# First MoE: token rows fetched from DRAM by index, and output rows carried to the tokens through DRAM

## The chip, the cores and the metric

One Trainium2 chip, one NeuronCore. The metric is the device time of one execution in microseconds (us), the median of three runs. Engines are called as in the profile: PE (TensorE), DVE (VectorE), ACT (ScalarE), POOL (GpSimd), SP (the engine that issues the weight loads).

## What is computed

A two-block network on 256 tokens of width 1024; the second block also carries 256 context tokens. Each layer of the second block ends in a mixture of experts (MoE). The change is in the first of the two, which works on all 512 tokens:

```python
def moe(h, router_w, router_b, w_gate, w_up, w_down):   # 16 experts, hidden width 512, 2 experts per token
    scores = jax.nn.sigmoid(t @ router_w)
    ...                                                 # best group of 4 experts, the best 2 in it
    wts = wts / jnp.sum(wts, axis=-1, keepdims=True)
    def expert(acc, p):
        wg, wu, wd, gate_col = p
        y = (jax.nn.silu(t @ wg) * (t @ wu)) @ wd
        return acc + gate_col[:, None] * y, None
```

The gate and up weights of one expert are 1024x512 f32 each (2 MB), its down weights 512x1024 (2 MB): 96 MB for the 16 experts, all read from DRAM once.

## The kernel before

Only the tokens that chose an expert are sent through it. `route` and `plan` score the tokens, order the experts by their load and give each token a slot number in each expert that it chose. The work is cut into tiles of 128 slots. A tile "B" is one expert with 128 slots; a tile "P" is a pair of experts with 64 slots each. `ORDER` lists the 12 tiles of this MoE (`BBBPBPBPBPBB`), and two neighbours make a unit: B B, four times B P, B B. An expert with more tokens than slots gets further rounds in a branch (`overflow`), which all engines pass between `plan` and the first unit.

For each unit:
- `gather`: DVE writes one-hot matrices `m_oh` (token by slot). For each of 8 chunks of 128 features, PE multiplies them with the normalised tokens, which are kept as a rounded part `m_xh` and a rest `m_xl`: 8 x 4 x 2 = 64 matmuls of 256 columns. ACT and DVE bring the result to `m_u0` and `m_u1`. Eight small matmuls with `m_w2` give the weight of each slot (`m_wsl`).
- `hidden`: gate and up products (PSUM `up`). A B tile splits its weights into a rounded part and a rest on ACT (L249, `phi`) and DVE (L250, `plo`) and takes three products (`acc3`); a P tile multiplies in full f32 straight from the loaded weights `wraw`. Four transposes turn the result.
- `down`, `down2`: the down product (PSUM `pd`) and `outputs`, which scales it into `m_y`, again as a rounded part and a rest.
- `combine`: two matmuls with `m_sP` and two DVE compares make the transposed one-hot `m_ot`; `scatter` multiplies it with `m_y` (32 matmuls of 512 columns), and 16 DVE operations add the result to the tokens `xl` and `xc` (L2067).

Weights come in 1 MB loads on SP's queue (`wraw`) into a ring of six buffers; a buffer is free again when it has been split (B) or multiplied (P). The loop over the jobs (one for each tile) runs `hidden` of job n, `combine` of the unit that is done, `gather` of the next unit, then `down` of job n-1. A scheduler puts the instructions of each engine in a fixed order when the program is built; it interleaves these groups on PE, but each engine then runs in that order.

Of the kernel before, what the change touches and what calls it, by code (L numbers as in the profile page):

```python
# [6 lines left out]
F32 = mybir.dt.float32  # L7
F32R = mybir.dt.float32r
I32 = mybir.dt.int32
AF = mybir.ActivationFunctionType  # L10
OP = mybir.AluOpType
AX = mybir.AxisListType
# [3 lines left out]
NCH = 8  # L16
# [136 lines left out]
class Kern:  # L153
# [1547 lines left out]
    def plan(self, asg, sc, nt, mp):  # L1701
# [3 lines left out]
        N = 128 * nt  # L1705
# [54 lines left out]
        for j in range(nt):  # L1760
            self.mm(pv[:, 16 * j:16 * j + 16], wT[:, 128 * j:128 * j + 128], pm.bitcast(F32), True, True)
        w2 = mp.tile([128, nt, 16, 2], F32R, name="m_w2")
        pv = pv[:, :16 * nt].rearrange("p (a b) -> p a b", b=16)
# [37 lines left out]
    def moe(self, l, seqs):  # L1801
# [30 lines left out]

        y = self.big0.tile([128, 2, 2, 1024], F32R, name="m_y")
        xh = self.big0.tile([128, nt, 1024], F32R, name="m_xh")
        xl = self.big0.tile([128, nt, 1024], F32R, name="m_xl")
# [36 lines left out]

        st = {"n": 0}
        for j in range(nt):
            s, ts = j // 2, slice(128 * (j % 2), 128 * (j % 2) + 128)
            for q in range(2):
                n = 2 * j + q
                tp = self.pp.tile([128, 512], F32, name="aux" if n in (4, 5) else "mm", bufs=3 if n in (4, 5) else 4)
                sl = slice(512 * q, 512 * q + 512)
                for i in range(4):  # L1880
                    self.mm(tp[:, 128 * i:128 * i + 128], seqs[s][0][:, 4 * q + i, ts], gain[:, s, 4 * q + i], i == 0, False)
                self.mm(tp, ri[:, j % 2, s], shift[:, s, sl], False, True)
                st["xh"] = nc.scalar.activation(xh[:, j, sl], tp, AF.Copy, scale=rk[:, s, j % 2:j % 2 + 1])
                if l == 0 and n < 6:
                    v = mp.tile([128, 512], F32, name="m_xv", bufs=2)
                    nc.scalar.activation(v, tp, AF.Copy, scale=rk[:, s, j % 2:j % 2 + 1])
                    nc.gpsimd.tensor_tensor(xl[:, j, sl], v, xh[:, j, sl].bitcast(F32), OP.subtract)
                else:
                    nc.vector.scalar_tensor_tensor(xl[:, j, sl], tp, rk[:, s, j % 2:j % 2 + 1], xh[:, j, sl].bitcast(F32), op0=OP.mult, op1=OP.subtract)
        idr = mp.tile([16, 16], F32R, name="m_idr")  # L1890
        nc.vector.tensor_copy(idr, C["ident"][:16, :16])
# [46 lines left out]
        def gather_(oh, u):  # L1938
# [7 lines left out]
            for c in range(NCH):  # L1946
# [9 lines left out]
                for t in range(n):  # L1956
# [4 lines left out]
                    if not all(plain):  # L1961
                        nc.vector.tensor_tensor(xs[t][:, c], xs[t][:, c], xp[:, 1, t], OP.add)
            wps = aux()[:, :8 * n].rearrange("p (t w) -> p t w", t=n)
            wsl = mp.tile([128, 2], F32, name="m_wsl", bufs=2)
            for t, es in enumerate(u):
                for j in range(nt):
                    self.mm(wps[:, t, :2 * len(es)], oh[:, j, t], w2[:, j, es[0]:es[0] + len(es)].rearrange("p a b -> p (a b)"), j == 0, j == nt - 1)
                k = 128 // len(es)
                for e in range(len(es)):
                    nc.vector.tensor_reduce(wsl[k * e:k * e + k, t:t + 1], wps[k * e:k * e + k, t, 2 * e:2 * e + 2], AX.X, OP.add)  # L1970
            return wsl

        def gather(u):
            oh = mp.tile([128, nt, 2, 128], F32R, name="m_oh")
            for t, es in enumerate(u):
                n, k = len(es), 128 // len(es)
                if n > 1:
# [4 lines left out]
            return gather_(oh, u)  # L1982

# [37 lines left out]
        def outputs(pds, t, wsl):  # L2021

            yo, ws = y[:, t], wsl[:, t:t + 1]
            for z in range(2):
                cs = slice(512 * z, 512 * z + 512)
                nc.scalar.activation(yo[:, 0, cs], pds[z], AF.Copy, scale=ws)  # L2026
                nc.vector.scalar_tensor_tensor(yo[:, 1, cs], pds[z], ws, yo[:, 0, cs].bitcast(F32), op0=OP.mult, op1=OP.subtract)  # L2027

        up_ps()
# [27 lines left out]
        def scatter(ot):  # L2057

            for c in range(NCH):
                op = aux()  # L2060
                n = 0
                for i, o in enumerate(ot):
                    for v in range(2):
                        self.mm(op[:, :N], y[:, i, v, 128 * c:128 * c + 128], o, n == 0, n == 2 * len(ot) - 1)
# [56 lines left out]
        ws = gather(units[0])  # L2121
        st["late"], st["n"] = (st["xh"], st["oh"]), 0
        pend = done = None
# [28 lines left out]

    def run_all(self):
        with self.wpool(3) as self.wp, self.tc.tile_pool(name="xp", bufs=1, reuse_waits="tile") as self.xp:
            with self.tc.tile_pool(name="mwp", bufs=1, reuse_waits="tile") as self.mwp:
# [4 lines left out]
        with self.wpool(3) as self.wp:  # L2160
            self.layer2()
        self.moe_consts()
        with self.wpool(6) as self.wp, self.phase() as self.big0, self.phase() as self.big:
            self.moe(0, [(self.xl, 0), (self.xc, 1)])
# [36 lines left out]
```

## Time and profile before

| | |
|---|---|
| time, median of 3 runs | 2230.29 us (2228.47 to 2234.14) |
| profiled execution | 2234.03 us, span 2232.3 us |
| PE busy in the span | 2122.1 us (95%) |
| DVE busy | 1429.5 us (64%) |
| ACT busy | 1007.4 us (45%) |
| POOL busy | 72.7 us (3%) |
| DMA | 425.12 MB moved, mean 190 GB/s |

The span runs from the first to the last instruction of the profiled execution; what lies around it makes 1.7 us more. Busy shares are means over stages with different limits: the first MoE is one such stage, and the rows below are read from it.

### The profile page before, as it was taken

Reading aid. Unit: us, or ns where it says so; the run is one execution under the profiler, and the core shown is the slowest. Engines: PE = TensorE matmul, PEld = TensorE weight load, DVE = VectorE, ACT = ScalarE, POOL = GpSimd, SP = SyncE. Lnnn points to the kernel's source line nnn. Section 1 sums busy time; section 2 is a strip of 40 time slices with the busy share of each in tenths; the row PEclk is TensorE's granted clock in tenths of the full one; section 3 lists DMA queues with packets and bytes.
Section 4 is the critical chain, followed back from the end, with each engine's and each line's share of the span. In section 5 each row is a group of like instructions: output and inputs, shape, how many; then the busy total and the mean of one; then the engine's idle time right before and its main releaser. Section 6 shows DMA issues by size and latency. Waiting matters only on the chain. (4 is left out here: it accounts for less than half of the span.)

```text
span 2232.3 us, 34618 instructions
## 1 busy us (share of the span) xinstructions
PE 2122.1 (95%) x13602; PEld 1648.4 (74%) x13602; DVE 1429.5 (64%) x2749; ACT 1007.4 (45%) x1769; POOL 72.7 (3%) x131
## 2 busy tenths in 40 slices
PE   7999999999999999999799899999989999989997
PEld 6999788678998778778567587655678899754442
DVE  5886566657876789999774476543767678631222
ACT  5564534445555454555433474332546465221111
POOL 0100100110100000000000100000000000000000
PEclk9999989999999999999899999999999999989999
DMA  7765753546645222211012368888634343469996
GB/s 276 268 256 191 257 188 119 210 166 232 241 158 187 81 67 76 67 57 48 21 38 76 124 234 310 321 320 299 235 122 141 97 151 106 152 265 394 425 395 246
DMA packets 78166, 425.12 MB, mean 190 GB/s; under 512 B 12256, under 2 KB 14048, under 8 KB 38048
## 3 DMA queue, kind: packets, MB, share of 16 engines
q1 hardware_dynamic: 74912, 422.32, 51.6%
q8 instruction: 110, 1.80, 0.3%
q0 software_dynamic: 3072, 0.40, 0.1%
q14 instruction: 72, 0.59, 0.1%
HBM read 421.24 MB, written 1.05 MB: 189 GB/s over the span
## 5 line engine op out<-in xcount | busy, mean ns | idle before, releaser
L197 PE MATMUL mm<-act_x,whi 128*128 128x256 f32 x2048 | 383.5, 287 | 0.9 <-DVE act_x L352 0.4
L197 PEld LDWEIGHTS mm<-act_x,whi 128*128 128x128 f32 x2048 | 323.4, 193 | 22.9 <-issue 18.6
L197 PE MATMUL mm<-act_x,wlo 128*128 128x256 f32 x1024 | 292.1, 286 | 0.8 <-DVE wlo L228 0.8
L197 PE MATMUL mm<-act,phi 128*128 128x512 f32 (+2 forms) x816 | 264.4, 399 | 6.3 <-ACT phi L249 3.5
L228 DVE TENSOR_TENSOR wlo<-wraw,whi 128x2048 fp32r<-128x2048 f32 (+1 forms) x101 | 208.3, 2063 | 88.8 <-ACT whi L227 88.4
L227 ACT CAST whi<-wraw 128x2048 fp32r<-128x2048 f32 (+1 forms) x101 | 173.7, 1720 | 178.8 <-PE mm L197 133.8
L250 DVE TENSOR_TENSOR plo<-wr,phi 128x1024 fp32r<-128x1024 f32 (+2 forms) x146 | 159.2, 1095 | 103.7 <-ACT phi L249 102.1
L249 ACT CAST phi<-wr 128x1024 fp32r<-128x1024 f32 (+2 forms) x146 | 137.4, 943 | 194.3 <-PE mm L197 165.0
L197 PEld LDWEIGHTS mm<-act_x,wlo 128*128 128x128 f32 x1024 | 197.7, 193 | 4.3 <-issue 2.7
L197 PEld LDWEIGHTS mm<-act,phi 128*128 128x128 f32 (+1 forms) x816 | 150.6, 189 | 46.5 <-issue 8.6
L197 PE MATMUL up<-wraw,m_u 128*64 128x512 f32 (+2 forms) x744 | 184.3, 596 | 0.0
L1038 DVE SCALAR_TENSOR_TENSOR uc<-up,fvt,uc 128x512 f32<-128x512 f32 x217 | 158.9, 746 | 7.5 <-ACT uc L1033 6.2
L197 PE MATMUL mm<-act,plo 128*128 128x512 f32 (+2 forms) x408 | 161.8, 398 | 0.0
L197 PE MATMUL mm<-act_x,phi 128*128 128x256 f32 x768 | 147.7, 292 | 3.5 <-ACT qs L1528 3.0
L197 PEld LDWEIGHTS up<-wraw,m_u 128*64 128x64 f32 (+2 forms) x744 | 58.9, 137 | 100.8 <-issue 100.0
L197 PEld LDWEIGHTS mm<-act_x,phi 128*128 128x128 f32 x768 | 124.1, 198 | 7.8 <-ACT qs L1528 3.2
L250 DVE TENSOR_TENSOR plo<-wraw,phi 128x1024 fp32r<-128x1024 f32 x96 | 114.3, 1221 | 11.6 <-ACT phi L249 10.4
L249 ACT CAST phi<-wraw 128x1024 fp32r<-128x1024 f32 x96 | 99.2, 1055 | 43.6 <-DMA wraw<-in_moe_d_dram 14.9
L197 PE MATMUL mm<-act_x,plo 128*128 128x256 f32 x384 | 111.9, 292 | 2.1 <-DVE plo L250 2.0
L2008 DVE TENSOR_TENSOR m_g<-m_g,up 128x512 f32<-128x512 f32 x20 | 13.7, 687 | 135.5 <-PE up L197 135.5
L197 PE MATMUL mm<-hhi,whi 128*128 128x256 f32 x352 | 99.7, 284 | 0.0
L197 PE MATMUL mm<-hlo,whi 128*128 128x256 f32 x352 | 99.7, 284 | 0.0
(609 smaller groups left out, 4276.4 us busy)
## 6 DMA issues: line engine op xcount, KB each, us to landing
wraw<-in_moe_g_dram SPq DMA_DIRECT2D x64, 1024.0 KB, 6.8
wraw<-in_moe_u_dram SPq DMA_DIRECT2D x61, 1024.0 KB, 8.8
wraw<-in_moe_d_dram SPq DMA_DIRECT2D x61, 1024.0 KB, 9.1
wmod<-in_mod_w_dram SPq DMA_DIRECT2D x48, 1024.0 KB, 6.1
wraw<-in_ffn_up_dram SPq DMA_DIRECT2D x44, 1024.0 KB, 4.9
wr<-in_hg_in_dram SPq DMA_DIRECT2D x64, 512.0 KB, 3.9
wraw<-in_ffn_down_dram SPq DMA_DIRECT2D x32, 704.0 KB, 4.0
wraw<-in_ple_gate_dram SPq DMA_DIRECT2D x8, 1024.0 KB, 4.9
```

What stands on the lines that cost most here:

```text
L197: self.nc.tensor.matmul(out, lhsT, rhs, start=first, stop=last)
L227: nc.scalar.copy(hi, raw)
L228: nc.vector.tensor_tensor(lo, raw, hi.bitcast(F32), OP.subtract)
L249: self.nc.scalar.copy(hi, src)
L250: self.nc.vector.tensor_tensor(lo, src, hi.bitcast(F32), OP.subtract)
L1038: nc.vector.scalar_tensor_tensor(o, up[:, :, k:k + 64], self.fv("cf_w", 8 * k + b), o, op0=OP.mult, op1=OP.add)
L2008: nc.vector.tensor_tensor(sg, sg, u, OP.mult)
```

## The change

Only the first MoE changes (`rowed`). Two DRAM tensors are new: `xd` holds the 512 normalised tokens as rows of 4 KB, `yd` the output rows of the first ten tiles and one row of zeros.
- Ahead of the units, ACT writes each of the eight token pieces a second time in f32 (`m_xv`, two buffers; six pieces did so before) and POOL stores it to `xd`. DVE works out for each token the two rows of `yd` that will hold its outputs (`r_rowi`).
- `m_w2` has two more columns, a token number and zero, so that the eight small matmuls also give the token number of each slot.
- The first unit is gathered as before. For each later unit, `ask` makes the one-hot and the small matmuls one tile ahead and lets POOL fetch 128 token rows for each of its two tiles by an indirect transfer (`xg`, two buffers). `fetch` turns them with 16 PE transposes and splits (B) or copies (P) them to `m_u0` and `m_u1`.
- `outputs` of the first ten tiles writes f32 rows (`y0`, four buffers), and POOL stores them to `yd`. Their `combine` is gone. In the last job `collect` fetches for each block of 128 tokens the two rows of each token (eight indirect transfers), adds them on DVE, turns them with 32 transposes and adds them to `xl` and `xc`.
- The last unit keeps its `combine`.

The new tiles `xg`, `yg` and `y0` take the places of `m_xh`, `m_xl` and `m_y`. The diff, cut to its core:

```diff
-        w2 = mp.tile([128, nt, 16, 2], F32R, name="m_w2")
+        w2 = mp.tile([128, nt, 16, nt], F32R, name="m_w2")
+        if nt == 4:
+            tn = mp.tile([128, nt, 2], F32, name="r_tn")
+            nc.vector.memset(tn[:, :, 1], 0.0)
+            for j in range(nt):
+                nc.vector.tensor_scalar(tn[:, j, 0:1], self.pidx[:, 0:1], float(128 * j - self.SLOT), None, op0=OP.add)
+            nc.vector.tensor_copy(w2[:, :, :, 2:], tn[:, :, None].to_broadcast([128, nt, 16, 2]))
...
+        rowed = l == 0
+        if rowed:
+            xd = self.dram.tile([128 * nt, 1024], F32, name="xd")
+            yd = self.dram.tile([128 * (len(order) - 2) + 1, 1024], F32, name="yd")
+            none = 128 * (len(order) - 2)
...
-                if l == 0 and n < 6:
+                if rowed:
                     v = mp.tile([128, 512], F32, name="m_xv", bufs=2)
                     nc.scalar.activation(v, tp, AF.Copy, scale=rk[:, s, j % 2:j % 2 + 1])
-                    nc.gpsimd.tensor_tensor(xl[:, j, sl], v, xh[:, j, sl].bitcast(F32), OP.subtract)
+                    nc.gpsimd.dma_start(xd[128 * j:128 * j + 128, sl], v)
+                    (nc.gpsimd if n < 6 else nc.vector).tensor_tensor(xl[:, j, sl], v, xh[:, j, sl].bitcast(F32), OP.subtract)
...
+            nc.vector.tensor_tensor(e, slot, bc(1), OP.is_lt)
+            nc.vector.scalar_tensor_tensor(e, slot, float(self.SLOT), e, op0=OP.is_ge, op1=OP.mult)
+            nc.vector.tensor_tensor(v, slot, bc(0), OP.add)
+            nc.vector.tensor_tensor(v, v, e, OP.mult)
+            rows = mp.tile([128, 2, nt], F32, name="r_rows")
+            nc.vector.tensor_reduce(rows[:, 0], v, AX.X, OP.min)
+            nc.vector.tensor_tensor(e, v, rows[:, 0][:, :, None].to_broadcast([128, nt, 16]), OP.is_equal)
+            nc.vector.scalar_tensor_tensor(v, e, 1e5, v, op0=OP.mult, op1=OP.add)
+            nc.vector.tensor_reduce(rows[:, 1], v, AX.X, OP.min)
+            nc.vector.tensor_scalar(rows, rows, 0.0, float(none), op0=OP.min, op1=OP.add)
+            rowi = mp.tile([128, 2, nt], U32, name="r_rowi")
+            nc.vector.tensor_copy(rowi, rows)
...
+        def slots_(oh, u, idx=None):
+            n = len(u)
+            wps = aux()[:, :4 * nt * n].rearrange("p (t w) -> p t w", t=n)
...
                 for j in range(nt):
-                    self.mm(wps[:, t, :2 * len(es)], oh[:, j, t], w2[:, j, es[0]:es[0] + len(es)].rearrange("p a b -> p (a b)"), j == 0, j == nt - 1)
+                    self.mm(wps[:, t, :nt * len(es)], oh[:, j, t], w2[:, j, es[0]:es[0] + len(es)].rearrange("p a b -> p (a b)"), j == 0, j == nt - 1)
...
+            if idx is not None:
+                nc.vector.tensor_copy(idx, wps[:, :n, 2])
...
+        def ask(u):
+            ti = mp.tile([128, 2], U32, name="m_ti", bufs=2)
+            wsl = slots_(onehot(u), u, ti)
+            k = st["asked"] = st.get("asked", 1) ^ 1
+            for t in range(2):
+                nc.gpsimd.indirect_dma_start(xg[:, k, t], None, xd[:, :], bass.IndirectOffsetOnAxis(ap=ti[:, t:t + 1], axis=0))
+            return u, k, wsl
+        def fetch(asked):
+            u, k, wsl = asked
+            xs = []
+            for t, es in enumerate(u):
+                p = whole(es)
+                v = mp.tile([128, 1024 if l == 1 else 2048], F32 if p else F32R, name="m_u%d" % t)
+                v = v[:, :1024].rearrange("p (c n) -> p c n", c=NCH) if p else v.rearrange("p (c v n) -> p c v n", c=NCH, v=2)
+                xs.append(v)
+                for q in range(2):
+                    tp = aux()
+                    for i in range(4):
+                        c = 4 * q + i
+                        nc.tensor.transpose(tp[:, 128 * i:128 * i + 128], xg[:, k, t, 128 * c:128 * c + 128], C["ident"])
+                    tp = tp.rearrange("p (c n) -> p c n", c=4)
+                    o = v[:, 4 * q:4 * q + 4]
+                    if p:
+                        nc.scalar.copy(o, tp)
+                    else:
+                        self.split(o[:, :, 0], o[:, :, 1], tp)
+            st["x"] = xs
+            return wsl
...
-            yo, ws = y[:, t], wsl[:, t:t + 1]
+            ws = wsl[:, t:t + 1]
+            i = st["tile"]
+            st["tile"] += 1
+            if 0 <= i < len(order) - 2 and rowed:
+                yo = y0[:, i % 4]
+                nc.scalar.activation(yo[:, :512], pds[0], AF.Copy, scale=ws)
+                nc.vector.tensor_scalar(yo[:, 512:], pds[1], ws, None, op0=OP.mult)
+                nc.gpsimd.dma_start(yd[128 * i:128 * i + 128], yo)
+                return
+            yo = st["y"][:, t]
...
+        def collect():
+            for s_, (x, r) in enumerate(seqs):
+                for j in range(2):
+                    J = 2 * s_ + j
+                    for k in range(2):
+                        nc.gpsimd.indirect_dma_start(yg[:, j, k], None, yd[:, :], bass.IndirectOffsetOnAxis(ap=rowi[:, k, J:J + 1], axis=0))
+                    nc.vector.tensor_tensor(yg[:, j, 0], yg[:, j, 0], yg[:, j, 1], OP.add)
+                for q in range(4):
+                    tp = aux().rearrange("p (c j t) -> p c j t", c=2, j=2)
+                    for i in range(2):
+                        c = 2 * q + i
+                        for j in range(2):
+                            nc.tensor.transpose(tp[:, i, j], yg[:, j, 0, 128 * c:128 * c + 128], C["ident"])
+                        nc.vector.scalar_tensor_tensor(x[:, c], tp[:, i].rearrange("p j t -> p (j t)"), self.mvec(l, 5, c, r), x[:, c], op0=OP.mult, op1=OP.add)
...
+        if rowed:
+            xg, yg = (self.big0.tile([128, 2, 2, 1024], F32, name=v) for v in ("m_xh", "m_xl"))
+            y0 = self.big0.tile([128, 4, 1024], F32, name="m_y")
+            nc.gpsimd.memset(y0[0:1, 3], 0.0)
+            nc.gpsimd.dma_start(yd[none:none + 1], y0[0:1, 3])
+        pend = done = asked = None
         for n in range(len(jobs) + 1):
             if n < len(jobs):
                 u, t = jobs[n]
                 hd = hidden(u[t], t)
                 next(hd)
                 now, last = (u, t, ws), t + 1 == len(u)
+                if rowed and t == 0 and n + 2 < len(jobs):
+                    asked = ask(jobs[n + 2][0])
             if done:
                 combine(done)
                 done = None
+            if rowed and n == len(jobs) - 1:
+                collect()
             if n + 1 < len(jobs) and last:
-                ws = gather(jobs[n + 1][0])
+                ws = fetch(asked) if rowed else gather(jobs[n + 1][0])
             if pend:
                 (u_, t_, w_), hT, l_ = pend
+                if rowed and st["tile"] == len(order) - 2:
+                    st["y"] = self.big0.tile([128, 2, 2, 1024], F32R, name="m_y")
                 if whole(u_[t_]):
                     down2(u_[t_], hT, t_, w_)
                 else:
                     down(u_[t_][0], hT, t_, w_)
-                if l_:
+                if l_ and not (rowed and u_ is not units[-1]):
                     done = u_
```

## Rows read from the trace of the kernel before

**Rows 1.** Busy time of each engine in three stretches (the columns stand in its first line):

```profile
core 0: us, PE busy (x) PEld busy (x) DVE busy (x) ACT busy (x) POOL busy (x), PEclk, DMA share, GB/s
2040.00:2130.00 90.00, 89.84 (x392) 39.13 (x389) 14.64 (x32) 11.46 (x29) 0.00 (x0) 1.00 1.01 425
1436.80:1496.70 59.90, 59.90 (x286) 35.91 (x284) 29.82 (x50) 19.87 (x36) 0.00 (x0) 1.00 0.82 306
1592.00:1627.00 35.00, 33.58 (x146) 26.50 (x145) 32.37 (x49) 20.60 (x26) 0.00 (x0) 1.00 0.37 136
```

**Rows 2.** Timeline of PE: start, duration, instruction, count, idle time before and its releaser:

```profile
1282.37 1.01 PE L197 MATMUL aux<-m_oh,m_xh 128*128 128x256 f32 x3 [2.87 <-ACTq L2106]
...
1429.16 0.64 PE L197 MATMUL aux<-m_oh,m_xh 128*128 128x256 f32 x4
...
1436.83 0.50 PE L197 MATMUL aux<-m_w,m_oh 128*128 128x2 f32 x4
...
1443.22 0.60 PE L2012 MATMUL aux<-c_ident,m_g 128*128 128x128 f32 x4
1443.58 0.47 PE L197 MATMUL up<-phi,m_u 128*128 128x512 f32 x1
...
1454.93 7.09 PE L197 MATMUL pd<-wraw,m_hT 128*64 128x512 f32 x32
...
1466.12 0.49 PE L197 MATMUL aux<-m_sP,m_idr 16*128 16x512 f32 x1
...
1466.77 1.07 PE L197 MATMUL up<-wraw,m_u 128*64 128x512 f32 x2
...
1496.62 0.50 PE L197 MATMUL aux<-m_w,m_oh 128*128 128x2 f32 x4
...
1620.64 7.46 PE L197 MATMUL aux<-m_ot,m_y 128*128 128x512 f32 x32
1628.04 0.64 PE L197 MATMUL aux<-sq,c_ones 128*32 128x256 f32 x8
```

**Rows 3.** DMA issues from 1282 to 1640: count, KB of each, median us to landing:

```profile
wraw<-in_moe_g_dram SPq DMA_DIRECT2D x30, 1024.0 KB, 6.5
wraw<-in_moe_u_dram SPq DMA_DIRECT2D x30, 1024.0 KB, 6.7
wraw<-in_moe_d_dram SPq DMA_DIRECT2D x30, 1024.0 KB, 5.4
```

**Rows 4.** Timeline of SP's queue, first and last loads of one B P unit:

```profile
1432.82 14.54 SPq L214 DMA_DIRECT2D wraw<-in_moe_d_dram  x4
...
1488.82 1.17 SPq L214 DMA_DIRECT2D wraw<-in_moe_u_dram  x2
```

**Rows 5.** Two stretches of 5 us of the first MoE, columns as in the first group:

```profile
1282.00:1287.00 5.00, 4.63 (x22) 4.63 (x23) 3.32 (x3) 4.39 (x7) 0.14 (x1) 0.52 0.01 5
...
1307.00:1312.00 5.00, 5.00 (x23) 4.04 (x22) 4.65 (x6) 4.00 (x6) 0.00 (x0) 1.00 1.00 357
```

**Rows 6.** Groups of instructions from 1436.8 to 1496.7 (one B tile's splits):

```profile
L250 DVE TENSOR_TENSOR plo<-wraw,phi 128x1024 fp32r<-128x1024 f32 x12 | 14.4, 1224 | 2.0 <-ACT phi L249 1.7
```

**Rows 7.** Timelines of ACT, DVE and POOL ahead of the first unit:

```profile
1263.17 0.68 ACT L1886 ACTIVATE m_xv<-mm,r_rk 128x512 f32<-128x512 f32 x1
...
1270.99 0.57 ACT L1717 CAST m_g<-aux 16x512 fp32r<-16x512 f32 x1 [3.67 <-PE aux L197]
...
1280.12 0.68 ACT L1886 ACTIVATE m_xv<-aux,r_rk 128x512 f32<-128x512 f32 x1
...
1279.63 1.29 DVE L1980 TENSOR_TENSOR m_oh<-iot,r_slot 128x512 fp32r<-128x512 f32 x2 [2.69 <-PEq L2106]
...
1280.88 1.26 POOL L1887 TENSOR_TENSOR m_xl<-m_xv,m_xh 128x512 fp32r<-128x512 f32 x1 [1.46 <-ACT m_xv L1886]
```

**Rows 8.** Groups of instructions on POOL: its own DMA issues:

```profile
L825 POOL DMA_DIRECT2D mrows<-md x96 | 49.6, 523 | 506.9 <-ACT md L819 483.6 <-ACT apt L740 23.3
```

**Rows 9.** DMA queues (packets, MB, share of 16 engines) and issues, whole span:

```profile
q0 software_dynamic: 3072, 0.40, 0.1%
...
mrows<-md POOLq DMA_DIRECT2D x96, 4.0 KB, 5.3
...
out_dram<-xl SPq DMA_DIRECT2D x4, 256.0 KB, 2.1
```

More of the change, by code (lines that the diff above doesn't have):

```diff
@@ L9 @@
 I32 = mybir.dt.int32
+U32 = mybir.dt.uint32
 AF = mybir.ActivationFunctionType
@@ L1833, in moe @@
         y = self.big0.tile([128, 2, 2, 1024], F32R, name="m_y")
+        rowed = l == 0
[3 more added lines that the diff above has]
+            none = 128 * (len(order) - 2)
+            rc = mp.tile([128, 2, 16], F32, name="r_rc")
+            nc.gpsimd.memset(rc, 0.0)
+            for i, es in enumerate(order[:-2]):
+                k = 128 // len(es)
+                for e, r in enumerate(es):
+                    nc.gpsimd.memset(rc[:, 0, r:r + 1], float(128 * i + k * e - self.SLOT - none))
+                    nc.gpsimd.memset(rc[:, 1, r:r + 1], float(self.SLOT + k))
         xh = self.big0.tile([128, nt, 1024], F32R, name="m_xh")
@@ L1871, in moe @@
         slot, sP, w2, idx = self.plan(asg, sc, nt, mp)
-        st = {"n": 0}
+        st = {"n": 0, "y": y, "tile": -10000}
         for j in range(nt):
@@ L1883, in moe @@
                 st["xh"] = nc.scalar.activation(xh[:, j, sl], tp, AF.Copy, scale=rk[:, s, j % 2:j % 2 + 1])
-                if l == 0 and n < 6:
+                if rowed:
                     v = mp.tile([128, 512], F32, name="m_xv", bufs=2)
                     nc.scalar.activation(v, tp, AF.Copy, scale=rk[:, s, j % 2:j % 2 + 1])
-                    nc.gpsimd.tensor_tensor(xl[:, j, sl], v, xh[:, j, sl].bitcast(F32), OP.subtract)
+                    nc.gpsimd.dma_start(xd[128 * j:128 * j + 128, sl], v)
+                    (nc.gpsimd if n < 6 else nc.vector).tensor_tensor(xl[:, j, sl], v, xh[:, j, sl].bitcast(F32), OP.subtract)
                 else:
                     nc.vector.scalar_tensor_tensor(xl[:, j, sl], tp, rk[:, s, j % 2:j % 2 + 1], xh[:, j, sl].bitcast(F32), op0=OP.mult, op1=OP.subtract)
+        if rowed:
+            v, e = (mp.tile([128, nt, 16], F32, name="r_v%d" % i) for i in range(2))
+            bc = lambda i: rc[:, i:i + 1].to_broadcast([128, nt, 16])
+            nc.vector.tensor_tensor(e, slot, bc(1), OP.is_lt)
[10 more added lines that the diff above has]
+            nc.vector.tensor_copy(rowi, rows)
         idr = mp.tile([16, 16], F32R, name="m_idr")
@@ L1962, in gather_ @@
                         nc.vector.tensor_tensor(xs[t][:, c], xs[t][:, c], xp[:, 1, t], OP.add)
-            wps = aux()[:, :8 * n].rearrange("p (t w) -> p t w", t=n)
+            return slots_(oh, u)
+        def slots_(oh, u, idx=None):
+            n = len(u)
+            wps = aux()[:, :4 * nt * n].rearrange("p (t w) -> p t w", t=n)
             wsl = mp.tile([128, 2], F32, name="m_wsl", bufs=2)
@@ L1966, in gather_, with onehot @@
                 for j in range(nt):
-                    self.mm(wps[:, t, :2 * len(es)], oh[:, j, t], w2[:, j, es[0]:es[0] + len(es)].rearrange("p a b -> p (a b)"), j == 0, j == nt - 1)
+                    self.mm(wps[:, t, :nt * len(es)], oh[:, j, t], w2[:, j, es[0]:es[0] + len(es)].rearrange("p a b -> p (a b)"), j == 0, j == nt - 1)
                 k = 128 // len(es)
                 for e in range(len(es)):
-                    nc.vector.tensor_reduce(wsl[k * e:k * e + k, t:t + 1], wps[k * e:k * e + k, t, 2 * e:2 * e + 2], AX.X, OP.add)
+                    nc.vector.tensor_reduce(wsl[k * e:k * e + k, t:t + 1], wps[k * e:k * e + k, t, nt * e:nt * e + 2], AX.X, OP.add)
+            if idx is not None:
+                nc.vector.tensor_copy(idx, wps[:, :n, 2])
             return wsl
-        def gather(u):
+        def onehot(u):
             oh = mp.tile([128, nt, 2, 128], F32R, name="m_oh")
@@ L1976, in gather @@
                 n, k = len(es), 128 // len(es)
-                if n > 1:
+                if n > 1 and not (rowed and u is not units[-1]):
                     sel = sels[es[0]] = mp.tile([16, 128], F32R, name="m_sel", bufs=4)
@@ L1981, in gather @@
                                         slot[:, :, es[0]:es[0] + n][:, :, :, None].to_broadcast([128, nt, n, k]), OP.is_equal)
-            return gather_(oh, u)
+            return oh
+        def gather(u):
+            return gather_(onehot(u), u)
+        def ask(u):
[26 more added lines that the diff above has]
+            return wsl
         def proj(n, rs, t):
@@ L2063, in scatter @@
                     for v in range(2):
-                        self.mm(op[:, :N], y[:, i, v, 128 * c:128 * c + 128], o, n == 0, n == 2 * len(ot) - 1)
+                        self.mm(op[:, :N], st["y"][:, i, v, 128 * c:128 * c + 128], o, n == 0, n == 2 * len(ot) - 1)
                         n += 1
@@ L2121, in moe @@
         ws = gather(units[0])
-        st["late"], st["n"] = (st["xh"], st["oh"]), 0
-        pend = done = None
+        st["late"], st["n"], st["tile"] = (st["xh"], st["oh"]), 0, 0
+        if rowed:
+            xg, yg = (self.big0.tile([128, 2, 2, 1024], F32, name=v) for v in ("m_xh", "m_xl"))
[3 more added lines that the diff above has]
+        pend = done = asked = None
         for n in range(len(jobs) + 1):
@@ L2153, in run_all @@
     def run_all(self):
+        ctx_ = self.ctx
         with self.wpool(3) as self.wp, self.tc.tile_pool(name="xp", bufs=1, reuse_waits="tile") as self.xp:
@@ L2162, in run_all @@
         self.moe_consts()
+        self.dram = ctx_.enter_context(self.tc.tile_pool(name="dram", bufs=1, space=bass.MemoryType.DRAM))
         with self.wpool(6) as self.wp, self.phase() as self.big0, self.phase() as self.big:
```

## The prediction

> **What bounds the kernel now.** The busy shares of the page say little here, so I read the first MoE by stretches of time. In a middle B P unit PE is busy 59.90 of 59.90 us, DVE 29.82, ACT 19.87, and the DMA engines 0.82 of the time at 306 GB/s [rows 1]: PE is the bound, and DMA comes second, at four fifths. The reader is to see how near the second limit lies: in the last MoE of the kernel the DMA engines are full (share 1.01) and move 425 GB/s [rows 1], so the weights of the first MoE could come at most 1.4 times as fast as now. The timeline of PE gives the stage's ends: the first gather starts at 1282.37, the last combine ends at 1628.04 [rows 2], 345.7 us. In the last unit a third engine matters: DVE is busy 32.37 of 35 us [rows 1].
>
> **What PE loses.** A gather is 64 matmuls from 1429.16 to 1436.83, 7.67 us; five go: 38.4 us. A combine is 32 matmuls from 1620.64 to 1628.04, 7.40 us, and two ahead of it from 1466.12 to 1466.77, 0.65 us; five go: 40.3 us [rows 2]. In their place stand 5 x 16 + 32 = 112 transposes; four take 0.36 us (1443.22 to 1443.58 [rows 2]), so 10.1 us. By PE alone the stage would be 68.6 us shorter. The eight small matmuls of a unit stay.
>
> **What DMA then allows.** A B P unit lasts 59.8 us, from the end of one gather (1436.83) to that of the next (1496.62) [rows 2]. Without gather and combine, with 16 transposes, PE needs 59.8 - 7.67 - 8.05 + 1.44 = 45.5 us. In it SP issues 18 loads, six rows of its timeline of which the first and the last stand above [rows 4], of 1024 KB each [rows 3]: 18.9 MB. The change adds two indirect transfers of 128 rows of 4 KB, 1.05 MB, and two stores of 0.52 MB: 21.0 MB in all. At the 425 GB/s of [rows 1] this takes 49.4 us, longer than PE. So the unit turns from PE-bound to DMA-bound and keeps part of the gain only. The rate while loads wait for buffers is lower: a full 5 us stretch (share 1.00) moved 357 GB/s while a B tile freed one buffer at a time [rows 5]. That gives 58.8 us, and PE alone gives the other end, 45.5. I take 410 GB/s, nearer to 425, because a P tile frees its buffers faster than DMA fills them: 51.2 us, a gain of 8.6 us in each of the four B P units, 34.4 us (4.0 at 357 GB/s, 57.2 by PE alone).
>
> **The first and the last unit** are B B: 12 loads, 12.6 MB, fewer bytes for each us of PE, so PE keeps its gain where it is the bound. The gather at the end of the first unit becomes a fetch: 7.67 - 1.44 = 6.2 us. In the last unit a combine becomes `collect`. DVE, which bounds this unit, keeps its 16 additions into the tokens and gets four additions of 128x1024, each about the 1.22 us of a split of that size [rows 6], so nothing is gained there. Against it stands a new chain. The store of tile 9 is issued when its `down` ends. Then come, one after the other, four indirect transfers on POOL, two additions, transposes, and four more transfers into the same `yg` buffers, which can start only when the transposes have read them. No row times an indirect transfer. POOL's own DMA issue takes 523 ns [rows 8] for 32 packets (3072 over 96 issues) and lands after 5.3 us [rows 9]; 128 rows by the same rate for each packet would be 2.1 us. So one is 0.52 to 2.1 us to issue. The chain is 6 us of store, twice four issues, twice 5.3 us of landing and about 6 us of additions and turning: 27 to 39 us. It has as cover the up products of the last tile (11.4 us, 1443.58 to 1454.93 [rows 2]), two down products and what stands between, some 24 us: 3 to 15 us uncovered. If PE took the transposes in program order, ahead of the two downs, it could be 26; if all hides, nothing. I take 10.
>
> **Ahead of the units** each `m_xv` buffer now stays held until its store has landed. The nearest rows are 2.1 us for 256 KB from SP and 5.3 us for POOL's own [rows 9]. Eight pieces share two buffers, so ACT, which is in order, waits: the copies at 1263.17 and behind have slack, since ACT stood idle 3.67 us before 1270.99, but the later ones run up to 1280.12, POOL's last subtraction behind them to 1282.1, and the engines then pass the overflow branch to the first gather [rows 7]. Behind ACT are the copies of the slot plan and the branch. Two more copies and up to three waits for a store give 0 to 8 us; I take 4. The twelve small DVE operations for `r_rowi`, the six for `m_w2` and POOL's memsets I cost at nothing: DVE stands idle 2.69 us at that branch [rows 7], POOL is idle long before; without this cover they are about 3 us, inside the 8.
>
> **Costed at nothing:** `ask` (DVE one-hots that existed before), the splits of `fetch` (fewer and larger operations than before), SP's queue (no new issues), the ten stores on POOL (idle there). A wait for rows on POOL holds back only later stores and fetches. Rows asked for one tile ahead have the next tile's up products and a down as cover, at least 11.4 + 5.8 us; their chain (one-hot, small matmuls, two issues, 5.3 us landing) is 9 to 13 us. I add 1 us for TensorE's clock: after the idle 2.87 us ahead of the first gather [rows 2] the granted clock was 0.52 for 5 us [rows 5], and waits for weights may repeat that; most of it falls into time that PE would wait in anyway.
>
> **The sum:** -34.4 - 6.2 + 10 + 4 + 1 = -25.6 us. The profiled execution, 2234.03 us (span 2232.3 and 1.7 around it), becomes 2208.4. It stands 3.7 us above the median of the runs, 2230.29, so I forecast a median of 2205. What this kernel's runs can tell from no change is about 0.3%, 6.7 us.
>
> **Rivals.**
> - *PE stays the bound.* The ring of six loads and the split buffers even out the rates, and the B B units lend their spare DMA time. For it: the mean of the whole stage asks for less than 425 GB/s even after the change. Against: six loads are one third of a unit's. Then -57.2 - 6.2 + 10 + 4 = -49.4, or 2181.
> - *Mixed traffic runs at 357 GB/s,* the low row of [rows 5]. Then B P units gain 4.0 in all and the sum is -4.0 - 6.2 + 15 = +4.8: 2235, the same. Against: 90 us at 425 [rows 1].
>  The Trainium skill, "SBUF — State Buffer", Summary: rules for kernel authors, says to reckon HBM to SBUF transfers at about 358 GB/s. By it the unit would take 58.7 us and the sum come out at +4; the trace disagrees, with 425 GB/s measured. Its page "HBM Reference", Access, says that a core streaming alone measures about 425, and the trace agrees.
> - *POOL's indirect transfers are slow (slower than before).* They are the one operation without a row. Their place is `collect`, where eight stand in series at the end. The tail costs about 8X - 2 us for X us each; it eats the whole gain and 6.7 us more from X = 5.5. At X = 7 the tail is 54 instead of 10, the sum +18, the time 2248. Against: 0.52 us for the nearest row.
> - *The rows come late.* Indirect transfers queue behind megabyte loads, and PE waits 4 us at each of the five fetches: +20, 2225. Against: the cover of 17 us.
>
> **How the numbers follow.** Chances: forecast 0.48 (its own range 2190 to 2218), PE-bound 0.17, 357 GB/s 0.12, slow indirect transfers 0.13, late rows 0.10. The range leaves out the slow transfers and a few hundredths of the tails: 2176 to 2236. Faster by over 0.3%: 0.48 + 0.17, half of the late rows and a little of the rest, 0.72. Within: 0.12. Slower: 0.13 and part of the 357 GB/s, 0.16.
>
> **What would show it.** Right: in the B P units a DMA share near 1 at over 400 GB/s, PE with gaps of some us in front of `wraw` matmuls, and units of about 51 us; the first gather some 4 us later; a wait of PE or DVE for `yg` near the end. Wrong: units near 45 us with PE full, or a DMA share of 1 at a low rate; POOL issues of several us each; gaps in front of the transposes of `fetch`. A different order of the engines' queues, which the trace of before can't show, would move single terms.

## The result, and the profile after

The changed kernel takes 2247.77 us (median of four runs, 2243.96 to 2248.78) beside 2229.38 for the kernel before on the same chip: ratio 1.0069 [1.0053, 1.0086], slower by 0.7%. The forecast was 2205 with a range of 2176 to 2236. The profiled execution took 2243.96 us (span 2242.2).

The stage now runs from 1288.27 to 1641.10, 352.8 us against 345.7 [rows 2]. That is 7.1 us of the some 15 us (0.0069 of 2229) that the kernel lost; the rest came ahead of the first gather. Two executions don't reach this stage at the same time after their start, so the way to the first gather is counted from the last addition of the layer before, which is the same instruction in both kernels. DVE before, then DVE after:

```profile
1252.97 0.48 DVE L1292 SCALAR_TENSOR_TENSOR xl<-mm,mt,xl 128x256 f32<-128x256 f32 x1
```

```profile
1249.48 0.47 DVE L1293 SCALAR_TENSOR_TENSOR xl<-mm,mt,xl 128x256 f32<-128x256 f32 x1
```

From there the first gather starts after 29.4 us before (1282.37) and after 38.8 us now (1288.27): 9.4 us more. Timeline of PE after the change, columns as in [rows 2]:

```profile
1288.27 0.98 PE L198 MATMUL aux<-m_oh,m_xh 128*128 128x256 f32 x3 [10.84 <-DVE m_oh L2027]
...
1398.79 0.61 PE L198 MATMUL aux<-m_w,m_oh 128*128 128x8 f32 x4 [1.19 <-DVE m_wsl L2015]
1399.33 1.08 PE L198 MATMUL up<-wraw,m_u 128*64 128x512 f32 x4
...
1412.67 1.30 PE L2056 MATMUL aux<-c_ident,m_xh 128*128 128x128 f32 x5 [9.69 <-DMA m_xh<-xd,m_ti]
...
1471.80 1.33 PE L2056 MATMUL aux<-c_ident,m_xh 128*128 128x128 f32 x5 [9.84 <-DMA m_xh<-xd,m_ti]
...
1533.34 1.33 PE L2056 MATMUL aux<-c_ident,m_xh 128*128 128x128 f32 x5 [9.58 <-DMA m_xh<-xd,m_ti]
...
1600.96 1.11 PE L2133 MATMUL aux<-c_ident,m_xl 128*128 128x128 f32 x4 [10.27 <-DVE m_xl L2127]
...
1641.10 0.64 PE L198 MATMUL aux<-sq,c_ones 128*32 128x256 f32 x8
```

The gathers and combines are gone, but PE stands 9.6 to 9.8 us in front of the transposes of three fetches, 10.3 us in front of the collected rows, and 10.8 us ahead of the first gather (2.87 before). What these waits do to the neighbours shows in four stretches of 20 us, columns as in [rows 1]:

```profile
1360.00:1380.00 20.00, 16.63 (x77) 9.91 (x74) 9.99 (x11) 10.32 (x14) 0.00 (x0) 1.00 1.01 425
1400.00:1420.00 20.00, 10.31 (x44) 4.29 (x42) 2.54 (x4) 1.17 (x2) 2.29 (x2) 0.74 0.75 293
1460.00:1480.00 20.00, 10.16 (x40) 4.75 (x38) 1.52 (x3) 1.17 (x2) 1.98 (x2) 0.66 0.71 286
1520.00:1540.00 20.00, 10.42 (x40) 4.90 (x41) 1.62 (x4) 1.17 (x2) 2.32 (x3) 0.74 0.78 309
```

Ahead of the first of the three waits the transfers reach 425 GB/s; in the stretches of 20 us between the waits, from 1420 to 1460 and from 1480 to 1520, they move 363 to 383. In each stretch with a wait PE works half the time, and its granted clock is 0.66 to 0.74 on the mean (a mixture of its two levels, 1.2 and 2.4 GHz, after the idle time). The transfers fall to 286 to 309 GB/s there: SP's loads wait for PE to free their buffers. From 1300 to 1560 SP waits for PE's up products for 93.9 us in all and 17.3 at the longest; in a later run without the waits (e14) it is 71.1 and 7.5.

Why are the rows late? DVE and POOL ahead of the first of these waits, two timelines:

```profile
1397.73 0.75 DVE L2111 TENSOR_SCALAR m_y<-pd,m_wsl 128x512 f32<-128x512 f32 x1 [2.37 <-PE pd L198]
1398.58 0.16 DVE L2015 TENSOR_REDUCE m_wsl<-aux 128x1 f32<-128x2 f32 x1
1399.44 0.33 DVE L2015 TENSOR_REDUCE m_wsl<-aux 64x1 f32<-64x2 f32 x2 [0.70 <-PE aux L198]
1399.80 0.16 DVE L2017 CAST m_ti<-aux 128x2 uint32<-128x2 f32 x1
...
1399.01 0.56 POOL L2112 DMA_DIRECT2D yd<-m_y  x1 [18.36 <-DVE m_wsl L2015]
1400.71 1.32 POOL L2040 DMA_INDIRECT m_xh<-xd,m_ti  x1 [1.14 <-issue]
1402.34 0.97 POOL L2040 DMA_INDIRECT m_xh<-xd,m_ti  x1 [0.30 <-issue]
```

The reduce that writes the weights of the next unit's slots (`m_wsl`) stands right behind the last output of the unit before (`m_y`, which reads that unit's `m_wsl`). The tile has two buffers, and a third unit is asked for while two still need theirs. Behind the reduce come four small matmuls, the row numbers (`m_ti`), and two indirect issues. PE, in its fixed order, goes 16 matmuls (3.6 us) into the next tile's up products and then wants the rows: at 1402.98 (1412.67 - 9.69), while POOL is still issuing the second transfer (1402.34 to 1403.31). The DMA issues of the whole span (KB, median us to landing):

```profile
yd<-m_y POOLq DMA_DIRECT2D x10, 512.0 KB, 8.6
xd<-m_xv POOLq DMA_DIRECT2D x8, 256.0 KB, 2.6
...
m_xh<-xd,m_ti POOLq DMA_INDIRECT x10, 11.9
m_xl<-yd,r_rowi POOLq DMA_INDIRECT x8, 5.3
```

Beside the weight loads the rows take 11.9 us to land; at the end of the stage, where the loads run out (135 GB/s from 1600 to 1620), the same number of bytes takes 5.3.

### The profile page after: what moved, and what is told of

Read it like the earlier page. It is cut to its first block, busy times and chain, and to the rows that moved or that the text cites. A ratio compares the mean times of both kernels' runs of the same rounds, so it can differ in the third digit from the quotient of the medians.

```text
span 2242.2 us, 33778 instructions
## 1 busy us (share of the span) xinstructions
PE 2066.5 (92%) x13224; PEld 1596.4 (71%) x13224; DVE 1396.4 (62%) x2666; ACT 992.3 (44%) x1701; POOL 106.3 (5%) x198
## 3 DMA queue, kind: packets, MB, share of 16 engines
q1 hardware_dynamic: 74912, 422.32, 51.2%
```

## The experiments

Theories at the start: **T1**, rows asked too late make the loss; **T2**, the weights' queue is the bound anyway and a removed wait only becomes a wait for weights (**D** further down); **T3**, the tail and the front cost it. All ratios are to the kernel before on the same chip.

**1. The ask earlier in the program (e1), and each half of the change alone (e2, e3, e4).** e1 calls `ask` behind the `fetch` of the unit before:

```
-                if rowed and t == 0 and n + 2 < len(jobs):
-                    asked = ask(jobs[n + 2][0])
+                if rowed and n == 0:
+                    asked = ask(jobs[2][0])
...
                 ws = fetch(asked) if rowed else gather(jobs[n + 1][0])
+                if rowed and n + 3 < len(jobs):
+                    asked = ask(jobs[n + 3][0])
```

> The changed kernel with one edit: the rows of the unit after next are asked for right after the rows of the next unit are fetched, so about a whole unit (some 45 us) ahead of their transposes instead of some 12 us. Nothing is left out. Late rows (T1): the three waits of 9.69, 9.84 and 9.58 us before the fetches go, with the half-rate clock and the starved weight queue behind them, and the time falls by 29 us or more, to 2205 to 2219. DMA-bound units (T2): the waits for rows only turn into waits for weights, and the time stays within 8 us of the 2247.8 of the changed kernel. Cost in the tail and front (T3): likewise about 2240 to 2250, with the 10.3 us wait of the collect and the 10.8 us wait of the first gather still there.

1.0068 [1.0045, 1.0092], 2248.35 us: nothing changed, and PE still waited 30.5 us for fetched rows. T1 in this form falls, but not in favour of T2, for the waits did not move. The timeline of DVE in this run shows why:

```profile
1454.97 0.75 DVE L2111 TENSOR_SCALAR m_y<-pd,m_wsl 128x512 f32<-128x512 f32 x1 [2.31 <-PE pd L198]
1455.82 0.16 DVE L2015 TENSOR_REDUCE m_wsl<-aux 128x1 f32<-128x2 f32 x1
...
1457.04 0.16 DVE L2017 CAST m_ti<-aux 128x2 uint32<-128x2 f32 x1
```

Asked a whole unit earlier in the program, the reduce still stands behind the same output. Not the place of the ask holds it but the buffer that it writes.

The halves: e2 keeps the gathers and sends the outputs through DRAM; e3 fetches rows and keeps the combines; e4 is e3 with the edit of e1.

```
e2:   -                ws = fetch(asked) if rowed else gather(jobs[n + 1][0])
      +                ws = gather(jobs[n + 1][0])
e3:   -            if 0 <= i < len(order) - 2 and rowed:
      +            if False:
      -            if rowed and n == len(jobs) - 1:
      -                collect()
      -                if l_ and not (rowed and u_ is not units[-1]):
      +                if l_:
```

> Half of the change: token rows are gathered by matmul as in the kernel before, the outputs of five units go through DRAM and are collected. Nothing is left out. T1: five combines (40.3 us of TensorE) go, 32 transposes and one wait of about 10 us for the collected rows come, no fetch can be late, so 2229 - 40 + 3 + 10 = about 2202, at most 2215. T2: a unit then needs 21.0 MB in 51 us as well as 52 us of TensorE, so about 2215 to 2225. T3: the tail of the collect eats the gain, 2229 to 2240.

> The other half: token rows by indirect transfers as in the changed kernel, outputs scattered by matmul as in the kernel before. Nothing is left out. T1: gathers (38.4 us) go, transposes (7.5 us), the later first gather (6 us) and three or four waits of about 9.7 us with their slow clock come, so 2229 to 2245. T2: 2215 to 2230. T3: if the tail of the collect is the loss, this half is faster than before, 2205 to 2215.

> Rows half alone (as the run before) with the rows asked for a whole unit ahead. Nothing is left out. T1: the waits of the fetches go, so 25 us or more below the rows half with late asking, 2200 to 2212. T2 (queue bound): within 8 us of the rows half with late asking. T3: the same as that run, 2205 to 2215.

Outputs alone: 0.9923 [0.9904, 0.9942], 2215.94 us. Rows alone: 0.9981 [0.9971, 0.9992], 2228.42; asked earlier: 0.9978 [0.9964, 0.9992], 2226.25. By their times all three lie where T2 had put them; T1 missed the outputs half by 1 us and the rows half with the early ask by 14, and its waits did not appear in the rows half. Neither half is slower than before, and both together are: the loss lies in how they meet. The outputs half reaches its first gather as fast as the kernel before (29.4 us from the last addition), the rows half 9.3 us later (38.7); so T3 holds for the front of the rows half, and the tail of the outputs half lies inside a run that is faster. Rows alone showed no wait for rows at a fetch, though asked as late. PE in that run, around the ask whose first transfer POOL issued at 1406.29:

```profile
1404.38 0.61 PE L198 MATMUL aux<-m_w,m_oh 128*128 128x8 f32 x4
...
1406.78 0.50 PE L198 MATMUL aux<-m_sP,m_idr 16*128 16x512 f32 x1
...
1426.11 0.28 PE L2033 MATMUL aux<-c_ident,m_xh 128*128 128x128 f32 x1
```

The combine of the unit before and the up products among it fill the 20 us between the ask and the transposes. That combine is what the other half of the change takes away.

**2. Three buffers for the slots' weights (e5)**, and on top of them the collect issued all at once (e6), eight places for the stored pieces (e7), and all three (e8).

```
e5:  -            wsl = mp.tile([128, 2], F32, name="m_wsl", bufs=2)
     +            wsl = mp.tile([128, 2], F32, name="m_wsl", bufs=3)
e6:  +            for J in range(4):
     +                for k in range(2):
     +                    nc.gpsimd.indirect_dma_start((yg, xg)[J // 2][:, J % 2, k], None, yd[:, :], ...)
     (adds and transposes after the last unit's first down)
e7:  -                    v = mp.tile([128, 512], F32, name="m_xv", bufs=2)
     +                    v = xv[:, n]
```

> The changed kernel with one number changed: the tile that holds the slots' weights (m_wsl) gets three buffers for two. Nothing is left out. Theory L (the ask waits for this buffer): with two buffers the ask of unit u+1 can't write its weights before the last outputs of unit u-1 have read theirs, so it came at most 14 us ahead of its transposes; with three it is issued some 30 us earlier, the four waits for fetched rows (30.1 us) go, and with them the half-rate clock behind three of them: 2205 to 2219. Rival D (the weights' queue bounds the units, the waits for rows only hide waits for weights): 2238 to 2250, with 20 us or more of waits for wraw. Rival S (the rows are late because their transfers stand behind the output stores in the same queue and share the bandwidth): half of the waits stays, 2230 to 2240.

> The run before (three weight buffers) and one more edit: all eight collecting transfers are issued together, the second sequence's into the tile of the fetched rows, and their adds and transposes come after the last unit's first down projection. Nothing is left out. Theory L with a tail cost: the wait of 10.3 us and that of 2.0 us for the collected rows go and the time falls 8 to 14 us below the run before. If those waits only stand in for work that TensorE must wait for anyway (weights of the last unit), it stays within 4 us.

> Three weight buffers, and the eight pieces of the token rows that are stored each in a place of its own (in the tile of the outputs, idle then) in place of two in turn. Nothing is left out. If the two pieces held the front by their stores, ScalarE no longer waits 1.24 and 0.75 us for them, and the first gather comes 2 to 4 us earlier than 1288.27; the time falls by 2 to 4 us below three buffers alone. If the front is late for the extra store and copies alone, no change.

> All three edits together: three weight buffers, the collect ahead, eight pieces. Nothing is left out. Theory L: the sum of the three, 2190 to 2208, below the outputs half alone (2215.9). Rival D: 2215 or more.

e5: 0.9954 [0.994, 0.9967], 2221.57 us: one number gives back 1.15%, some 26 us. The row numbers of the third fetch are now ready at 1374.34, and its transposes come at 1398.08 without a wait (timelines of DVE, POOL and PE):

```profile
1374.18 0.16 DVE L2017 CAST m_ti<-aux 128x2 uint32<-128x2 f32 x1
...
1375.08 1.83 POOL L2040 DMA_INDIRECT m_xh<-xd,m_ti  x1 [20.34 <-issue]
...
1398.08 0.60 PE L2056 MATMUL aux<-c_ident,m_xh 128*128 128x128 f32 x4
...
1449.86 0.38 PE L2056 MATMUL aux<-c_ident,m_xh 128*128 128x128 f32 x2
...
1501.00 0.71 PE L2056 MATMUL aux<-c_ident,m_xh 128*128 128x128 f32 x5
```

From fetch to fetch a B P unit lasts 51.8 and 51.1 us, where the changed kernel had 59.1 and 61.5 (1412.67, 1471.80, 1533.34). Theory L (the buffer) holds; S (the output stores in the same queue) is not needed, D not refuted yet: PE now waits 9.8 us for `wraw`, in seven places.

e6: 0.995 [0.9937, 0.9963], no clear gain (a miss): the engines' order still put the transposes amid the last tile's up products, where PE waited 10.6 us. e7: 0.9931 [0.9916, 0.9945], 5 us below e5 by the ratios, whose intervals overlap a little; the wait ahead of the first gather falls from 10.8 to 7.6 us, and the first gather comes 1.9 us earlier (37.0 us from the last addition, for 38.9 in e5). e8: 0.9925 [0.9912, 0.9938], 2215.61 us, no better than e7: theory L's 2190 to 2208 is missed, and the time is where rival D had put it.

**3. Which resource bounds the units (e9, e10).** A load that nobody needs, 256 KB, beside every second load of the up projections' weights:

```
+            if l == 0 and k0 == 0 and n != "moe_d":
+                nc.sync.dma_start(mp.tile([128, 512], F32, name="m_xv", bufs=2), A["moe_d"][0, 0, :, 0, :512])
             return self.wraw(A[n][l, ...])
```

> Three weight buffers (2221.6 in its run), and a needless load of 256 KB beside every second load of the two up projections' weights: 30 in all, 7.86 MB, 18.5 us at the 425 GB/s that the queue reached. The results are not changed. If the units are bound by the weights' queue once the rows come in time, the time rises by 12 to 20 us. If TensorE still binds them, by less than 5.

> The kernel before with the same 30 needless loads. If its units are bound by TensorE, as the prediction read them, it takes them with less than 5 us; if it is bound by the queue already, it rises by 12 to 20 as the run before does.

The kernel before takes the 7.86 MB for nothing: 1.0005 [0.9994, 1.0017]. With three buffers the ratio is 0.9977 [0.9967, 0.9987], 5 us over e5: on the whole time neither of the two expectations. The fetches of e9 (timeline of PE) tell where:

```profile
1391.62 0.27 PE L2058 MATMUL aux<-c_ident,m_xh 128*128 128x128 f32 x1
...
1447.01 0.27 PE L2058 MATMUL aux<-c_ident,m_xh 128*128 128x128 f32 x1
...
1502.32 0.27 PE L2058 MATMUL aux<-c_ident,m_xh 128*128 128x128 f32 x1
```

Units of 55.4 and 55.3 us, 3.6 and 4.2 longer than e5's; six such loads are 1.57 MB, 3.7 us at 425 GB/s. These units are bound by the queue. The units ahead had room: from the first gather (1288.56 in e9, 1291.96 in e5) to the third fetch e9 took 103.1 us and e5 106.1.

**4. The tail (e11, e12).** All eight collecting transfers at once, their adds and transposes held behind the last tile's hidden transposes; in the outputs half alone (e11) and in e8 (e12):

```
+            if rowed and n == len(jobs):
+                with tc.issue_after(st["tr"].ins), tc.issue_after(st["hid"][0].ins):
+                    collected()
```

> The outputs half alone (rows gathered by matmul; 2215.9 in its run), with all eight collecting transfers issued together and their adds and transposes held behind the last tile's hidden transposes, where their rows have landed. Nothing is left out. The wait of 8.8 us for the collected rows goes: 2205 to 2211. If that wait stands in for a later one (the last unit's weights, the clock), 2213 to 2217.

> The whole change with three weight buffers, eight pieces and the collect ahead (2215.6 in its run), and the collected rows' adds and transposes held as in the run before. Nothing is left out. The 9.2 and 3.6 us waits of the tail go: 2203 to 2210. If the rows half is worth anything beyond the outputs half, it is below the run before; if the queue bounds the units in both, the two are within 4 us.

e11: 0.988 [0.9862, 0.9898], 2205.68 us, the fastest kernel of the study. e12: 0.9895 [0.9878, 0.9911], 2209.37. PE's wait for collected rows falls from 8.8 to 2.6 us (e11) and from 9.2 and 3.6 to 1.9 (e12); the tail's wait was real: 0.0043 and 0.0030 by the ratios, some 10 and 7 us. On the whole time the rows half adds nothing to the outputs half: the two intervals overlap. The traces tell why: behind the first gather e12 is 6.3 us shorter (318.1 us to the end of the stage, for 324.4), and ahead of it 8.0 us longer (37.3 us from the last addition, for 29.3).

**5. The control (e13) and the cover (e14).** Whether the third buffer helped by time alone or by another order of PE's work: e13 has three buffers and holds the ask by hand behind the last output of the unit before; e14 keeps two buffers and the late ask, and in the four B P units moves the transposes behind all up products of the P tile in whose middle they stood.

```
e13: +                with tc.issue_after(st["out"].ins) if n else nullcontext():
     +                    asked = ask(jobs[n + 2][0])
e14: +                with tc.issue_after(st["up"].ins) if rowed and "up" in st else nullcontext():
                          ws = fetch(asked) if rowed else gather(jobs[n + 1][0])
```

> A control: three weight buffers, but the ask of the next unit is held by hand behind the last output of the unit before, where the two buffers had put it. Nothing is left out. If the time of the ask alone made the loss, the waits for fetched rows come back with about 8 to 10 us at each of three or four fetches, and the time is 2238 to 2252 though there are three buffers. If the third buffer helped in another way (the order of TensorE's work), it stays within 5 us of the 2221.6 with three buffers.

> The changed kernel with its two weight buffers and its late ask, but the transposes of the fetched rows are held behind all up matmuls of the tile in whose middle they stood (some 10 us later). Nothing is left out. If the loss is TensorE standing at rows that land 12 us after their ask, this cover takes most of the 30 us of waits away as the third buffer does: 2215 to 2228. If the late ask harms in another way, 2238 to 2250.

e13: 1.0036 [1.0025, 1.0048], 2239.37 us, with PE's waits for fetched rows back (6.9 to 7.7 us at three fetches, a little less than expected). e14: 0.9926 [0.9912, 0.9939], 2215.64 us, with no such wait. The waits of the two (one line each: us in total, times, longest; e14's longest kind in its place):

```profile
PE aux L2056 <- DMA m_xh<-xd,m_ti: 22.1, 4, 7.7
```

```profile
PE aux L2133 <- DVE m_xl L2127: 13.8, 2, 11.9
PE up L198 <- DMA wraw<-in_moe_u_dram: 13.3, 10, 2.6
```

The time of the ask against the place of its transposes makes this loss; the buffer was what set the time. From the changed kernel to e14 the ratio falls by 0.0143, 32 us, and what moved was one group of transposes in each B P unit, by some 10 us.

## Why the prediction was wrong, point by point

**The step that failed** is under "Costed at nothing": rows "asked for one tile ahead have the next tile's up products and a down as cover, at least 11.4 + 5.8 us". I read the ask's place from the loop and not what it has to wait for. Its `m_wsl` has two buffers, so it starts when the unit before has written its last output. And the transposes stand 16 matmuls into the next tile's up products, not behind them. The cover was 4.4 us (reduce at 1398.58, PE at the transposes by 1402.98) and the chain 14.1 us (to 1412.67), of which 11.9 is the landing that I took as 5.3. The 17.2 us that I counted would still have hidden that chain; the 4.4 did not. With the combine kept, a late ask stays hidden behind it (e3), and so it does behind other work (e14); the change takes the combine away and puts nothing in its place.

**The rival "the rows come late"** was the right one, at 0.10 and mis-sized: 4 us at each of five fetches against 9.7 at three and 30.1 in all, worth 26 us by e5 and 32 by e14. The text counted half of it as faster. Its reason, transfers behind megabyte loads, is the smaller part: the chain came out 1 to 5 us longer than forecast and the cover 12.8 us shorter, and in e5 the transfers still take 9.1 us to land and make PE wait 0.6 us in all. The measured 2247.8 is the number of another rival, slow indirect transfers at 7 us each (2248); that is chance, since they took 1.1 to 1.2.

**A second step failed beside it, the term for the front:** +4, with bounds of 0 to 8, where 9.4 us came (29.4 to 38.8 us from the last addition).

With the rows in time, the terms of the sum can be judged, by e14. Ends of the first gather, of the first and the last fetch and of the stage (timeline of PE), first before, where a gather stands for a fetch and the stage ends at 1628.04 [rows 2]:

```profile
1292.09 0.28 PE L197 MATMUL aux<-m_w,m_oh 128*128 128x2 f32 x2
...
1323.49 0.28 PE L197 MATMUL aux<-m_w,m_oh 128*128 128x2 f32 x2
...
1558.53 0.39 PE L197 MATMUL aux<-m_w,m_oh 128*128 128x2 f32 x3
```

then in e14 the last addition (DVE) and the instruction behind each of these ends (PE):

```profile
1248.63 0.47 DVE L1293 SCALAR_TENSOR_TENSOR xl<-mm,mt,xl 128x256 f32<-128x256 f32 x1
...
1297.42 0.51 PE L198 MATMUL aux<-m_w,m_oh 128*128 128x4 f32 x4
...
1323.58 0.47 PE L198 MATMUL pd<-phi,m_hT 128*128 128x512 f32 x1
...
1419.66 0.72 PE L198 MATMUL pd<-phi,m_hT 128*128 128x512 f32 x2
1470.83 0.49 PE L198 MATMUL pd<-phi,m_hT 128*128 128x512 f32 x1
1521.59 0.48 PE L198 MATMUL pd<-phi,m_hT 128*128 128x512 f32 x1
...
1608.17 0.42 PE L198 MATMUL aux<-sq,c_ones 128*32 128x256 f32 x4
```

| term | forecast | e14 against before |
|---|---|---|
| front, from the last addition | +4 | +9.7 (39.12 to 48.79) |
| first unit | -6.2 | -5.2 (31.40 to 26.16) |
| four B P units | -34.4 | -37.0 (235.04 to 198.01) |
| tail | +10 | +17.1 (69.51 to 86.58) |

From the last addition to the end of the stage it is -15.5 us (375.07 to 359.54) for the forecast -26.6 (without the 1 us for the clock); the runs of e14 say -16.5 (0.0074 of 2232). The 11 us between are the front and the tail, 5.7 and 7.1 us more than forecast; the units came out 1.6 us better. So even with the rows in time the kernel would have been at some 2215 (e14) and not at 2205. By the same measure the changed kernel stands at +16.5 us (391.62, 1249.48 to 1641.10): of the 43 us between this and the forecast the late rows are 32.

- *PE bound before:* right; e10 adds bytes for nothing.
- *DMA-bound units of 51.2 us at 410 GB/s:* right, though the changed kernel hid it. The last two B P units of e14 take 51.2 and 50.8 us (the first two 48.0 on the mean), and its middle stretch runs at 410 GB/s with a full queue:

```profile
1365.00:1520.00 155.00, 139.26 (x607) 73.52 (x603) 59.52 (x72) 52.65 (x67) 9.97 (x12) 0.97 1.01 410
```

 The same stretch of the kernel before moved 307 GB/s, of the changed kernel 362. The rival "PE stays the bound" falls with it, and so does "mixed traffic runs at 357 GB/s". The rule of the Trainium skill, "SBUF — State Buffer", Summary: rules for kernel authors (about 358 GB/s), again disagrees with the trace; "HBM Reference", Specifications (TRN2) (about 425 for a core alone; the prediction names the section Access), agrees, with 425 GB/s from 1360 to 1380 of the changed kernel.
- *Tail:* right in kind, 7 us short, inside its bounds of 0 to 26. PE waited 11.9 us for the first collected rows and ran at a granted clock of 0.66 from 1560 to 1580 of e14. Holding the transposes gets most of it back (e11, e12).
- *Front:* too small by more than half. The operations for `r_rowi`, costed at nothing, are free: the outputs half has them and stands at 29.4 us. The 9.4 us belong to what the rows half adds, the stores to `xd`, two more copies on ACT, and DVE's last two subtractions, which read these copies (DVE waits 5.7 us for the first of them). ACT waits twice for the stores, 1.24 and 0.75 us, and eight places take away 1.9 us (e7); how the other 7.5 us divide no run shows:

```profile
1280.13 0.69 ACT L1909 ACTIVATE m_xv<-mm,r_rk 128x512 f32<-128x512 f32 x1 [1.24 <-DMA xd<-m_xv]
1281.57 0.69 ACT L1909 ACTIVATE m_xv<-mm,r_rk 128x512 f32<-128x512 f32 x1 [0.75 <-DMA xd<-m_xv]
```

- *POOL's indirect transfers slow:* wrong. Groups of instructions on POOL (busy us, mean ns), from 1280 to 1645 of the changed kernel:

```profile
L2040 POOL DMA_INDIRECT m_xh<-xd,m_ti x10 | 10.8, 1085 | 31.7 <-DVE m_ti L2017 27.0 <-issue 4.7
L2126 POOL DMA_INDIRECT m_xl<-yd,r_rowi x8 | 9.7, 1214 | 21.8 <-issue 12.6 <-DVE m_xl L2127 4.9 <-PE aux L2133 4.3
```

 1.1 to 1.2 us each lies within the 0.52 to 2.1 of the text and far from the 5.5 from which they would have decided.
- *Clock:* +1 was too little as long as the rows were late, since each wait left PE at the lower level for a while; its share in the 32 us was not measured by itself.

Rows alone (e3) are only 0.2% faster for the same reason that e11 and e12 come out alike: behind the first gather e3 is 10.4 us shorter than before (335.2 for 345.7), and 9.3 of them are lost ahead of it. Still open is why the rows half gains only 10.4 and 6.3 us there, where five gathers less 80 transposes are some 31 us of PE by the prediction's figures. That this saving meets a queue that the bytes fill is argued from the DMA share of the middle stretch (0.94 in e2 and e11, 0.97 in e12, 1.01 in e14), not shown, and it does not fit e3, where the share is 0.88 and PE is busy 151.9 of 155 us.

## What to carry to other kernels

Before a transfer's wait is costed at nothing, follow its trigger back through every tile that the trigger writes: a small bookkeeping tile with one buffer too few can tie an early request to the end of old work, and moving the request in the program then changes nothing. When a change removes work, ask what that work was covering; two halves that are each harmless can lose together. Where an in-order engine waits, the cheapest cure can be to move the waiting instruction behind work that is ready. And compare a stage in two traces from an instruction that both share: the last addition ahead of this stage comes at 1252.97 in the kernel before and at 1247.39 in e10, whose source is the same up to there, and a difference of that size can hide a whole term.

## What the runs showed of the hardware that was not expected

- A POOL transfer of 128 indexed rows of 4 KB lands in 11.9 us beside the weight loads (9.1 in e5) and in 5.3 us where these run out; issuing it takes POOL 1.09 to 1.21 us, a plain store of the same size 0.57.
- The weight queue and POOL's own traffic together can still move as much as the weights alone (425 [rows 1]): 426 GB/s from 1420 to 1440 of e5, in which two indirect reads and a store are issued. Other stretches of 20 us with such traffic and a share of 0.99 moved less, 379 and 388 (1440 to 1460 and 1380 to 1400 of e14); what makes the difference is not shown.
- After an idle time of 9.7 us PE's granted clock over the 20 us around it was 0.66 to 0.74; in e5's stretches from 1400 to 1540, whose waits for weights are at most 2.6 us long, it was 0.91 to 1.00.
